# High and low weight parts in rows of eight instead of in turn, in an encoder block on one core

## The chip, the core and the metric

The kernel runs on one core of a Trainium2 chip. The metric is the device time of one execution in microseconds (us), as a median of several runs. The engines are named as the profile names them: PE is TensorE with its matmuls, PEld its weight loads, DVE is VectorE, ACT is ScalarE, POOL is GpSimd, SP is the queue that issues most transfers.

## The reference

One encoder layer on 256 tokens of width 2048, in f32, cut to the products that matter here:

```
h = rms_norm(x)
qa, ka, va, qb, kb, vb, ga, gb = split(h @ w_in)         # 2048 -> 10240 columns
ya = windowed attention(qa, ka, va)                       # 8 heads
yb = dilated attention(qb, kb, vb)                        # 12 heads, merged to 4
x  = x + (sigmoid(ga) * (ya @ w_branch_a) + sigmoid(gb) * (yb @ w_branch_b)) @ w_out
hf = rms_norm(x)
x  = x + (gelu(conv3(hf @ w_ffn_gate)) * (hf @ w_ffn_up)) @ w_ffn_down   # 2048 -> 5632 -> 2048
x  = x + sigmoid(rms_norm(x) @ w_ple_gate) * (p @ w_ple_proj)
out = rms_norm(x)
```

## The kernel before

**Two parts per number.** TensorE takes operands in a reduced f32 type here (`FR`), so each f32 operand is held as a high part and a low part, the low part being what the high part leaves over. A product of two such numbers is three matmuls: high by high, high by low, low by high.

**Two kinds of products.** In the first, weights are the moving operand (`wide_product`, L359 to L361, and `seven_product`, L410 to L412): 512 weight columns stream past a 128 by 128 block of activations. In the second kind, which the change concerns, a 128 by 128 weight block is the stationary operand and the activations move. For every block of weights `block` (L324 and L325) issues two matmuls into one PSUM accumulator `acc` of 128 by 512: the high part `whi` against 512 columns (256 tokens of the activations' high part, then 256 of their low part), and the low part `wlo` against the first 256 columns, added to the right half of `acc`. Later one ACT and one DVE operation (`gather`) add the halves. The left half is then high by high and the right half holds both mixed terms.

**Where that kind is used.** `product` does 16 blocks one after another for each head's query and key columns and for each 128 columns of the MLP's gate and up matrices. `products_by_halves` does the first three gate products together (`gg`): eight blocks of each of the three, then the other eight of each, so that half of the normalised input is enough to begin. Together these are 1840 blocks. Seven more products at the very start (tile `first`) call `block` themselves.

**How the weights come.** They lie in DRAM in the order of use. SP loads them in tiles of eight blocks (`raw`). `split_to` has ACT write `whi` (L261) and DVE write `wlo` (L262) for each tile of eight; there are four buffers of each. While the blocks of tile s are issued, `split_to(s + 3)` sees to it that tiles up to s + 2 are written in the program.

**What sets the order.** Each product has due times: `at((i, k), f)` puts a piece of other work (attention, norms, transposes) before block k of job i, and `run_due(i, k)` issues it there. So PE's order is that of the blocks with this other work between them; within ACT and DVE a scheduler that estimates durations orders what the program leaves free. The first product after the start is job `START` - 1, here called the first product; ahead of its block 6 stand the column sums for the first norm (L472), ahead of its block 12 the matmul that spreads the norm's factor over the partitions (L500, which needs POOL's power L486 and DVE's `rdg` L494). Transposes (`flip`, L878) turn the residual into the moving input `mov` (ACT L464, DVE L465); four of them lie in `gg` ahead of its blocks 8, 12, 16 and 20.

Of the kernel before, what the change touches and what calls it, by code (L numbers as in the profile page):

```python
# [17 lines left out]
T = 256  # L18
D = 2048
KC = D // P  # L20
# [17 lines left out]
SUB = 8  # L38
# [78 lines left out]
TOGETHER = 3  # L117
# [8 lines left out]
def _pairs(kind, c):  # L126

    if kind == "o":
        return ([2, 4, 5, 6, 7, 0, 1, 3] if c else [0, 1, 2, 4, 5, 6, 7, 3]), range(LATER, LATER + 4)
    if kind == "d1" and c == 1:  # L130
        return [5, 0, 1, 6, 2, 3, 7, 4, 8, 9, 10], range(5)
    return [8, 0, 1, 2, 3, 9, 4, 5, 6, 7, 10], range(SAVED)
# [34 lines left out]
def _whole(a):  # L167

    return _BLOCKS[a][0] == "w_out" or (_BLOCKS[a + SUB][1] % FHALF) // 2 in WHOLE
# [16 lines left out]
_SUB_OF = {a + o: (i, o) for i, (a, n, part) in enumerate(_SUBS) if not part for o in range(n)}  # L186
# [3 lines left out]
def _encoder(ctx: ExitStack, tc, xt, pt, cols, table, onehot, mask, ident_in, last_gain, wts, xrows, out):  # L190
    nc = tc.nc
# [34 lines left out]
    raws, subs = {}, {}  # L226
    pairs_of, kept = {}, {}
    state = {"raw": 0, "sub": 0, "at": 0, "back": 0}
# [12 lines left out]
    def load_all(i):  # L241
        while state["raw"] < min(i, 2 * _NPIECES):
            r, h = divmod(state["raw"], 2)
            seven = h and r * PIECE in _SEVEN
            load(r, h * SUB, h * SUB + (4 if seven else SUB))
            if seven and _whole(r * PIECE):
                nc.sync.dma_start(raws[2 * r + h][:, 4:, :], kept[_SEVEN.index(r * PIECE)][1])

    def split_to(i):
        while state["sub"] < min(i, len(_SUBS)):  # L250
            s = state["sub"]
            a, n, part = _SUBS[s]
            h, o = divmod(a, SUB)
            load_all(h + 6 + (part == 3))
            if part is None:
                src = raws[h][:, o:min(o + n, SUB), :]
            else:
                src = (raws[h + 1][:, :4, :], pairs_of.get(a), raws[h], raws[h + 1])[part]
            hi = wpool.tile(list(src.shape), FR, name="whi", bufs=4)
            lo = wpool.tile(list(src.shape), FR, name="wlo", bufs=4)  # L260
            nc.scalar.activation(hi, src, AF.Copy)  # L261
            ins = nc.vector.tensor_tensor(lo, src, hi.bitcast(F32), op=ALU.subtract)  # L262
            if _BLOCKS[a][0] in ("w_out", "w_ffn_down"):
                keep(ins)
            subs[s] = (hi, lo)
            state["sub"] = s + 1
            if part is not None:
                t2, t4 = raws[h + 1][:, 4:, :], raws[h + 1][:, :4, :]
            if part == 0 and not _whole(a):
                keep(nc.vector.tensor_tensor(t2, raws[h][:, :4, :], pairs_of[a][:, :4, :], op=ALU.subtract))  # L270
            if part == 1:
                keep(nc.vector.tensor_tensor(t4, raws[h][:, 4:, :], t2, op=ALU.subtract))
                j = _SEVEN.index(a)
                if all(not j <= e < j + 3 for e in _LAST):
                    back()
# [35 lines left out]
    def back():  # L311

        j = state["back"]
        t = pairs_of[_SEVEN[j]] = two_sums()
        nc.sync.dma_start(t, kept[j][0])
        state["back"] = j + 1

    def block(acc, m, first, last, ahead=3):

        b = state["at"]  # L320
        s, o = _SUB_OF[b]
        split_to(s + ahead)
        hi, lo = subs[s]
        nc.tensor.matmul(acc, hi[:, o, :], m, start=first, stop=False, skip_group_check=True)  # L324
        nc.tensor.matmul(acc[:, T:], lo[:, o, :], m[:, :T], start=False, stop=last, skip_group_check=True)  # L325
        state["at"] = b + 1
        if o == _SUBS[s][1] - 1:
            del subs[s]

    def product(i, moving, n):  # L330
        acc = ps.tile([P, 2 * T], F32, name="acc", bufs=3)
        for k in range(n):
            run_due(i, k)
            block(acc, moving(k), k == 0, k == n - 1)
        return acc

    def products_by_halves(i, moving):

        accs = []
        for b in range(TOGETHER * KC):  # L340
            (h, e), k = divmod(b // SUB, TOGETHER), b % SUB
            run_due(i, b)
            if h + k == 0:
                tag = "sp" if e < 2 else "acc"
                accs.append(ps.tile([P, 2 * T], F32, name="acc", tag=tag, bufs=2 if e < 2 else 3))
            block(accs[e], moving(SUB * h + k), h + k == 0, h == 1 and k == SUB - 1)
        return accs

    def wide_product(i, still, n, w, tag, places=HALVES, late=0):

        accs = [ps.tile([P, W4], F32, name="acc", tag=tag, bufs=3 if tag == "acc" else 2) for _ in places]

        def step(k, t, hi, lo):
            xh, xl = (still(k)[:, c:c + T][:, places[t]] for c in (0, T))
            acc = accs[t][:, :w * P]
            nc.tensor.matmul(acc, xh, hi, start=(k == 0), stop=False)  # L359
            nc.tensor.matmul(acc, xh, lo, start=False, stop=False)  # L360
            nc.tensor.matmul(acc, xl, hi, start=False, stop=(k == n - 1 - t * late))  # L361

        later = []
        for k in range(n):
            run_due(i, k)
            b = state["at"]
            s, o = _SUB_OF[b]
            split_to(s + 3)
            hi, lo = (m[:, o:o + w, :] for m in subs[s])
            step(k, 0, hi, lo)  # L370
            if k < n - late:
                step(k, 1, hi, lo)
            else:
                later.append((k, 1, hi, lo))
            state["at"] = b + w
            if o == _SUBS[s][1] - w:
                del subs[s]
        def rest(side=None):
            acc, c = (accs[1][:, :T], 0) if side is None else (side, T // P)
            for e, (k, t, hi, lo) in enumerate(later):  # L380
                xh, xl = (still(k)[:, c:c + T][:, places[t]] for c in (0, T))
                for i, (xs, ws) in enumerate(((xh, hi), (xh, lo), (xl, hi))):
                    nc.tensor.matmul(acc, xs, ws[:, c:c + T // P, :], start=(side is not None and e + i == 0),
                                     stop=(e + i == len(later) + 1), skip_group_check=True)
        return accs, rest
# [137 lines left out]
    def run_due(*i):  # L523
        for f, a in due.pop(i, []):
            f(*a)
# [48 lines left out]
    for step in order:  # L574
# [6 lines left out]
        while state["at"] < min(FIRST * ready, _SUBS[state["sub"]][0]):  # L581
            k, e = divmod(state["at"], FIRST)
# [15 lines left out]
    b = ps.tile([NH, 2 * T], F32, name="misc")  # L598
# [240 lines left out]
    def spread_sums(n, bank, end):  # L839

        u = row()
        nc.scalar.activation(u, bank["p1"], AF.Copy)  # L842
        to_residual(n, 0, 0, u)
        last = u
        for name in ("p6", "p7"):
            v = row()
            nc.vector.tensor_tensor(v, bank[name], last, op=ALU.add)
            last, u = v, last
        u, v = u, last
        to_residual(n, 1, 0, v)  # L850
        w = row()
        nc.vector.tensor_tensor(u, bank["p5"], u, op=ALU.add)
        nc.vector.tensor_tensor(w, bank["p5"], v, op=ALU.add)
        for t, a in enumerate((u, w)):
            if end:
                q = quarter(n, t, 1)
                nc.vector.tensor_tensor(q, q, a, op=ALU.add)
            else:
                to_residual(n, t, 1, a)
# [143 lines left out]
    for i, job in enumerate(_JOBS):  # L1003
        kind, n, _, _, _, blocks = job
# [79 lines left out]
        last = i == len(_JOBS) - 1  # L1084
        rest = None
        if kind == "v":
            far = n[0] >= KVH + HG
            acc, _ = wide_product(i, stills["v"], blocks, len(n), "acc", TWINS if far else HALVES)
        elif kind in ("o", "d0", "d1"):
# [5 lines left out]
            acc = seven_product(i, *_pairs(kind, n), still, lambda m, e: [a[:, e, :] for a in sums_at(m)], tags,  # L1095
                                lambda bank: spread_sums(n, bank, end))
        elif kind in stills:
            tag = {"pg": ("pt", "acc"), "pp": ("sp", "acc"), "gb": ("sp", "sp"), "ga": ("acc", "acc"), "ba": ("acc", "acc"),
                   "bb": ("sp", "sp" if n == 1 else "acc")}[kind][n % 2]
            acc, rest = wide_product(i, stills[kind], blocks, 4, tag, late=8 if last else 0)  # L1100
        elif kind == "gg":
            acc = products_by_halves(i, movers["g"])
        else:
            acc = product(i, movers[kind], blocks)
# [91 lines left out]
```

## Time and profile before

| what | value |
|---|---|
| median of 3 runs | 1469.22 us (1468.95 to 1469.9) |
| profiled execution, its own time | 1465.36 us |
| its span in the profile | 1463.6 us |
| granted TensorE clock, mean | 0.998 |
| PE busy | 1450.6 us, 99% of the span |
| weight loads busy | 1238.4 us, 85% |
| DVE busy | 1112.7 us, 76% |
| ACT busy | 816.2 us, 56% |
| traffic of the core's DMA engines | 362.17 MB, mean 247 GB/s |

A matmul's listed duration runs from its start to its modelled end, and matmuls overlap. What one costs the stream is therefore the step from its start to the start of the next one, not its listed duration. Such steps are read in the list of instructions in order of time, or from how many starts fall into a stretch in which PE does nothing else. The profiled execution is 3.86 us below the median of the timed runs.

### The profile page before, as it was taken

The numbers are of one execution on the slowest core, as the hardware profiler recorded it, in microseconds if no ns is written. First come the engines' busy times: TensorE is split into PE (matmuls) and PEld (weight loads), VectorE is DVE, ScalarE is ACT, GpSimd is POOL, SyncE is SP. The second block draws the span as 40 slices with busy tenths as digits, with TensorE's granted clock in tenths as the row PEclk, the third lists the DMA queues.
The fourth block names the chain that finished last, engine by engine and source line by source line (L and its number), as shares of the span: only waits on it lengthen the run. The fifth ranks groups of instructions, "written<-read, shape, count | busy, mean of one in ns | idle before, by whom it ended". The sixth has DMA issues, their size and how long they took to land.

```text
span 1463.6 us, 20762 instructions
## 1 busy us (share of the span) xinstructions
PE 1450.6 (99%) x7531; PEld 1238.4 (85%) x7531; DVE 1112.7 (76%) x1575; ACT 816.2 (56%) x1155; POOL 107.0 (7%) x178
## 2 busy tenths in 40 slices
PE   9999999999999999999999999999999999999997
PEld 8988888888888888788888887888888888788886
DVE  7686665665665668879888878897888876988665
ACT  7465444444444456666555555675555555666653
POOL 0000000001111100201011100102110100010000
PEclk9999999999999999999999999999999999999999
DMA  9654445557888977977788886989888874797652
GB/s 326 235 180 160 168 169 171 190 180 258 294 305 295 353 234 254 291 244 272 263 281 276 292 283 201 290 289 309 278 278 279 292 241 162 257 306 243 218 192 88
DMA packets 111730, 362.17 MB, mean 247 GB/s; under 512 B 12804, under 2 KB 17924, under 8 KB 111500
## 3 DMA queue, kind: packets, MB, share of 16 engines
q1 hardware_dynamic: 88908, 292.80, 58.2%
q0 software_dynamic: 20560, 63.71, 14.3%
q10 hardware_dynamic: 2160, 4.33, 0.9%
q8 instruction: 59, 0.97, 0.3%
q14 instruction: 43, 0.35, 0.1%
HBM read 324.06 MB, written 27.30 MB: 240 GB/s over the span
## 4 chain that ended last, share of the span: by engine, by line
PE 93%; DVE 1%; ACT 0%; issue 0%; POOLq 0%; POOL 0%; DVEq 0%
PE acc L324 28%; PE acc L325 14%; PE acc L360 9%; PE acc L359 9%; PE acc L361 9%; PE acc L411 7%; PE acc L410 7%; PE acc L412 7%; PE pt L685 1%; PE pt L878 0%; DVE wlo L262 0%; PE misc L700 0%; PE sp L644 0%; PE pt L900 0%; PE misc L631 0%
## 5 line engine op out<-in xcount | busy, mean ns | idle before, releaser
L262 DVE TENSOR_TENSOR wlo<-raw,whi 128x1024 fp32r<-128x1024 f32 (+2 forms) x556 | 650.9, 1182 | 289.2 <-ACT whi L261 284.2
L261 ACT ACTIVATE whi<-raw 128x1024 fp32r<-128x1024 f32 (+2 forms) x556 | 564.3, 1025 | 530.9 <-PE acc L324 191.0
L324 PE MATMUL acc<-mov,whi 128*128 128x512 f32 x1840 | 642.5, 394 | 0.0
L325 PE MATMUL acc<-mov,wlo 128*128 128x256 f32 x1840 | 514.2, 279 | 0.0
L324 PEld LDWEIGHTS acc<-mov,whi 128*128 128x128 f32 x1840 | 345.3, 188 | 76.9
L325 PEld LDWEIGHTS acc<-mov,wlo 128*128 128x128 f32 x1840 | 347.1, 189 | 0.3
L359 PE MATMUL acc<-whi,mov 128*128 128x512 f32 (+1 forms) x504 | 193.6, 384 | 0.0
L361 PE MATMUL acc<-whi,mov 128*128 128x512 f32 (+1 forms) x504 | 193.4, 384 | 0.0
L360 PE MATMUL acc<-wlo,mov 128*128 128x512 f32 (+1 forms) x504 | 193.3, 384 | 0.0
L359 PEld LDWEIGHTS acc<-whi,mov 128*128 128x128 f32 x504 | 95.2, 189 | 18.6 <-DVE first L452 0.5
L361 PEld LDWEIGHTS acc<-whi,mov 128*128 128x128 f32 x504 | 95.2, 189 | 18.5
L360 PEld LDWEIGHTS acc<-wlo,mov 128*128 128x128 f32 x504 | 95.2, 189 | 17.9
L410 PE MATMUL acc<-whi,act 128*128 128x512 f32 x207 | 80.9, 393 | 0.2 <-ACT whi L261 0.2
L411 PE MATMUL acc<-wlo,act 128*128 128x512 f32 x207 | 81.1, 392 | 0.0
L412 PE MATMUL acc<-whi,act 128*128 128x512 f32 x207 | 80.7, 390 | 0.0
L837 POOL DMA_DIRECT2D x<-row x36 | 31.0, 878 | 375.9 <-ACT row L842 255.3
L262 DVE TENSOR_TENSOR wlo<-sums,whi 128x1024 fp32r<-128x1024 f32 x37 | 45.2, 1220 | 8.5 <-ACT whi L261 8.4
L452 DVE TENSOR_TENSOR u<-acc,t 128x256 f32<-128x256 f32 x100 | 41.8, 418 | 8.4 <-ACT t L448 8.4
L410 PEld LDWEIGHTS acc<-whi,act 128*128 128x128 f32 x207 | 38.8, 188 | 9.4 <-ACT whi L261 1.5
L411 PEld LDWEIGHTS acc<-wlo,act 128*128 128x128 f32 x207 | 38.9, 188 | 9.2 <-DVE wlo L262 1.3
L411 PE MATMUL acc<-wlo,shl 128*128 128x512 f32 x116 | 45.7, 394 | 0.0
L412 PEld LDWEIGHTS acc<-whi,act 128*128 128x128 f32 x207 | 38.9, 188 | 7.9
(218 smaller groups left out, 1642.1 us busy)
## 6 DMA issues: line engine op xcount, KB each, us to landing
raw<-in_wts SPq DMA_DIRECT2D x477, 512.0 KB, 5.1
sums<-kept SPq DMA_DIRECT2D x37, 512.0 KB, 5.4
sums<-in_wts POOLq DMA_DIRECT2D x23, 512.0 KB, 7.9
kept<-sums POOLq DMA_DIRECT2D x23, 512.0 KB, 5.7
raw<-in_wts SPq DMA_DIRECT2D x39, 256.0 KB, 5.1
row<-in_wts POOLq DMA_DIRECT2D x37, 256.0 KB, 8.3
x<-row POOLq DMA_DIRECT2D x36, 256.0 KB, 7.6
two<-in_wts POOLq DMA_DIRECT2D x14, 512.0 KB, 8.2
```

The source lines that it names most:

```text
L261: nc.scalar.activation(hi, src, AF.Copy)
L262: ins = nc.vector.tensor_tensor(lo, src, hi.bitcast(F32), op=ALU.subtract)
L324: nc.tensor.matmul(acc, hi[:, o, :], m, start=first, stop=False, skip_group_check=True)
L325: nc.tensor.matmul(acc[:, T:], lo[:, o, :], m[:, :T], start=False, stop=last, skip_group_check=True)
L359: nc.tensor.matmul(acc, xh, hi, start=(k == 0), stop=False)
L360: nc.tensor.matmul(acc, xh, lo, start=False, stop=False)
L361: nc.tensor.matmul(acc, xl, hi, start=False, stop=(k == n - 1 - t * late))
L410: nc.tensor.matmul(acc, xh, hi, start=(e == 1), stop=False)
L411: nc.tensor.matmul(acc, xh, lo, start=False, stop=False)
L412: nc.tensor.matmul(acc, xl, hi, start=False, stop=(e == uses[name]))
L452: nc.vector.tensor_tensor(u, acc[:, :T], t, op=ALU.add)
L837: keep(nc.gpsimd.dma_start(quarter(n, t, c), a, accum_op=ALU.add))
```

## The change

`product` and `products_by_halves` no longer call `block` for each weight block. They call a new function `eight` for each tile of eight blocks. It issues the eight high matmuls and the eight low matmuls as two rows: for the first tile of a product high ones first, for a later tile low ones first. With 16 blocks to a product this gives 8 high, 16 low, 8 high, and since the next product begins with high again, rows of 16 of each in the middle of a stage. `eight` keeps due work at the same number of matmuls: it is called ahead of every second matmul, so what stood before block k of a tile now stands before the tile's matmul 2k. The products at the very start and both kinds with moving weights are as they were.

```diff
     def product(i, moving, n):
         acc = ps.tile([P, 2 * T], F32, name="acc", bufs=3)
-        for k in range(n):
-            run_due(i, k)
-            block(acc, moving(k), k == 0, k == n - 1)
+        for g in range(n // SUB):
+            eight(acc, lambda k: run_due(i, SUB * g + k), lambda k: moving(SUB * g + k), g == 0, g == n // SUB - 1)
         return acc

+    def eight(acc, due_at, moving, first, last):
+
+        s, _ = _SUB_OF[state["at"]]
+        for p in range(2 * SUB):
+            if p % 2 == 0:
+                due_at(p // 2)
+                split_to(s + 3)
+            hi, lo = subs[s]
+            k = p % SUB
+            m = moving(k)
+            if (p < SUB) == first:
+                nc.tensor.matmul(acc, hi[:, k, :], m, start=(first and k == 0), stop=(last and k == SUB - 1),
+                                 skip_group_check=True)
+            else:
+                nc.tensor.matmul(acc[:, T:], lo[:, k, :], m[:, :T], start=False, stop=False, skip_group_check=True)
+        state["at"] += SUB
+        del subs[s]
+
     def products_by_halves(i, moving):

         accs = []
-        for b in range(TOGETHER * KC):
-            (h, e), k = divmod(b // SUB, TOGETHER), b % SUB
-            run_due(i, b)
-            if h + k == 0:
+        for g in range(2 * TOGETHER):
+            h, e = divmod(g, TOGETHER)
+            if h == 0:
                 tag = "sp" if e < 2 else "acc"
                 accs.append(ps.tile([P, 2 * T], F32, name="acc", tag=tag, bufs=2 if e < 2 else 3))
-            block(accs[e], moving(SUB * h + k), h + k == 0, h == 1 and k == SUB - 1)
+            eight(accs[e], lambda k: run_due(i, SUB * g + k), lambda k: moving(SUB * h + k), h == 0, h == 1)
         return accs
```

The new lines move what follows down by 16: L472 becomes L488, L500 becomes L516, L465 becomes L481, and the two matmuls of `block` are L347 (high) and L350 (low) in these products.

In the first product PE's order before, around the column sums (`tot` holds the summed squares), is this:

```order
L324 MATMUL acc<-mov,whi 128x512
L325 MATMUL acc<-mov,wlo 128x256
L472 MATMUL misc<-ones,tot 128x1 x4
L324 MATMUL acc<-mov,whi 128x512
L325 MATMUL acc<-mov,wlo 128x256
```

In the changed kernel the same product, from its first matmul to the first rows of the next, stands so:

```order
L347 MATMUL acc<-mov,whi 128x512 x8
L350 MATMUL acc<-mov,wlo 128x256 x4
L488 MATMUL misc<-ones,tot 128x1 x4
L350 MATMUL acc<-mov,wlo 128x256 x12
L516 MATMUL misc<-rdg,ones 128x256
L347 MATMUL acc<-mov,whi 128x512 x16
```

The sums stand behind 8 high and 4 low matmuls instead of 6 and 6, and the spreading matmul behind 8 high and 16 low instead of 12 and 12.

In `gg`, PE's order in the changed kernel, with the four transposes (L894, L878 before) between the rows:

```order
L347 MATMUL acc<-mov,whi 128x512 x8
L350 MATMUL acc<-mov,wlo 128x256 x8
L894 MATMUL pt<-ident,x 128x128 x4
L347 MATMUL acc<-mov,whi 128x512 x8
L894 MATMUL pt<-ident,x 128x128 x4
L350 MATMUL acc<-mov,wlo 128x256 x8
L347 MATMUL acc<-mov,whi 128x512 x3
L894 MATMUL pt<-ident,x 128x128 x4
L347 MATMUL acc<-mov,whi 128x512 x5
L350 MATMUL acc<-mov,wlo 128x256 x4
L894 MATMUL pt<-ident,x 128x128 x4
L350 MATMUL acc<-mov,wlo 128x256 x18
```

The last transposes stand behind 24 high and 20 low matmuls, where before 20 high and 20 low ones stood ahead of them in this product; the row of 18 behind them takes 4 of its low matmuls from the third tile, 8 from the fourth and 6 from the fifth.

DVE's order around the same transposes, before (`mov` is the moving input, `rdg` the diagonal of the norm's factors):

```order
L262 TENSOR_TENSOR wlo<-raw,whi 128x1024 x2
L465 SCALAR_TENSOR_TENSOR mov<-pt,cl,mov 128x256 x4
L262 TENSOR_TENSOR wlo<-raw,whi 128x1024
L465 SCALAR_TENSOR_TENSOR mov<-pt,cl,mov 128x256 x4
L262 TENSOR_TENSOR wlo<-raw,whi 128x1024
L478 TENSOR_REDUCE sum<-marks 128x2
```

And in the changed kernel:

```order
L262 TENSOR_TENSOR wlo<-raw,whi 128x1024 x2
L481 SCALAR_TENSOR_TENSOR mov<-pt,cl,mov 128x256 x3
L262 TENSOR_TENSOR wlo<-raw,whi 128x1024
L481 SCALAR_TENSOR_TENSOR mov<-pt,cl,mov 128x256 x4
L262 TENSOR_TENSOR wlo<-raw,whi 128x1024
L481 SCALAR_TENSOR_TENSOR mov<-pt,cl,mov 128x256
```

The eighth piece of `mov` moved behind one more `wlo`. Elsewhere ACT and DVE keep the same instructions with some neighbours exchanged; POOL's order is the same, and SP's differs by the place of a few loads.

## The prediction

> **What bounds the kernel now.** I read the page's totals first, then the waits of PE, then PE's list in order of time, since the question is what one matmul costs the stream.
>
> ```profile
> span 1463.6 us, 20762 instructions
> PE 1450.6 (99%) x7531; PEld 1238.4 (85%) x7531; DVE 1112.7 (76%) x1575; ACT 816.2 (56%) x1155; POOL 107.0 (7%) x178
> PEclk9999999999999999999999999999999999999999
> L324 PE MATMUL acc<-mov,whi 128*128 128x512 f32 x1840 | 642.5, 394 | 0.0
> L325 PE MATMUL acc<-mov,wlo 128*128 128x256 f32 x1840 | 514.2, 279 | 0.0
> ```
>
> PE is busy from end to end at full clock, and the two matmuls of the change show no idle time ahead of them. So the kernel is as long as PE's stream of starts, and the change, which only reorders 3680 of PE's 7531 matmuls, must act through the steps between starts, or through new waits. The mean durations, 394 and 279 ns, are no steps: their ends are modelled and they overlap.
>
> ```profile
> 799.88 0.39 PE L324 MATMUL acc<-mov,whi 128*128 128x512 f32 x1
> 799.88 0.19 PEld L325 LDWEIGHTS acc<-mov,wlo 128*128 128x128 f32 x1
> 800.11 0.27 PE L325 MATMUL acc<-mov,wlo 128*128 128x256 f32 x1
> 800.11 0.19 PEld L324 LDWEIGHTS acc<-mov,whi 128*128 128x128 f32 x1
> 800.22 0.40 PE L324 MATMUL acc<-mov,whi 128*128 128x512 f32 x1
> ```
>
> In turn, high to low is 0.23 us and low to high 0.11 us, some 0.345 a pair. Each weight load starts together with the matmul before the one that uses it: the load for a high matmul lies beneath the short low one. For a mean over many pairs I count starts of L324 in stretches; the columns are the stretch, its length, PE's busy time with the count of starts, and the loads.
>
> ```profile
> core 0: us, PE busy (x) PEld busy (x), PEclk, DMA share, GB/s
> 186.00:210.00 24.00, 24.00 (x69) 12.80 (x68) 1.00 0.56 190
> 162.00:228.00 66.00, 50.16 (x142) 26.71 (x142) 1.00 0.50 168
> 246.00:284.00 38.00, 29.89 (x84) 15.82 (x84) 1.00 0.54 181
> 636.00:660.00 24.00, 19.81 (x55) 10.36 (x55) 1.00 0.57 201
> 1040.00:1200.00 160.00, 160.00 (x463) 86.50 (x462) 1.00 0.82 276
> ```
>
> In the MLP (last row) 160 us hold 463 starts, the one at the edge counted in, or 160 / 461.5 = 346.7 ns a pair. In a part of the head projections (first row) it is 24 / 68 = 353 ns, at the same clock and with less traffic: a slower rhythm of the same alternation, without any wait on another engine.
>
> **What the rows will cost.** The kernel already has both kinds of rows, each matmul with its own weight load: the last gate product runs 512 columns after 512, the first value product and the last gate's remainder 256 after 256. The first two lines are 36 steps apart, the next two 95, the next two 46, and the last two 95.
>
> ```profile
> 1439.99 0.39 PE L361 MATMUL acc<-whi,mov 128*128 128x512 f32 x1
> 1448.15 0.39 PE L361 MATMUL acc<-whi,mov 128*128 128x512 f32 x1
> ...
> 47.61 0.28 PE L360 MATMUL acc<-wlo,mov 128*128 128x256 f32 x1
> 59.00 0.40 PE L324 MATMUL acc<-mov,whi 128*128 128x512 f32 x1
> ...
> 1448.49 0.28 PE L383 MATMUL acc<-wlo,mov 128*128 128x256 f32 x1
> 1454.01 0.28 PE L383 MATMUL acc<-whi,mov 128*128 128x256 f32 x1
> ...
> 228.88 0.40 PE L359 MATMUL acc<-whi,mov 128*128 128x512 f32 x1
> 251.04 0.40 PE L361 MATMUL acc<-whi,mov 128*128 128x512 f32 x1
> ```
>
> A 512-column step is 8.16 / 36 = 226.7 ns. A 256-column step is 11.39 / 95 = 119.9 ns and 5.52 / 46 = 120.0 ns. Their sum is 346.7 ns, which is the alternating pair of the MLP to a tenth of a nanosecond. So a step's price goes by the matmul's own columns and not by its neighbour: 256 columns more cost 106.7 ns, and each matmul pays about 13.3 ns besides, in a row as in alternation. This is the core of the forecast: **rows cost what the turns cost**. (The last two lines, 22.16 / 95 = 233.3 ns, are a value product whose stationary operand takes every second column; they come back below.)
>
> One thing goes: if the rows run at 346.7 a pair everywhere, the slow rhythm ends. The three stretches that contain it hold 142, 84 and 55 high matmuls, at most 281 x (353 - 346.7) = 1.8 us; not all of them beat slowly, and I take **-1.6 us**. The bounds for the rhythm are -1.8 us and, were all 1840 high matmuls to step at 233.3, 1840 x 6.6 = +12.1 us. I take the near end, since of the 512-column rows the contiguous one, as the weight blocks here are, steps at 226.7.
>
> A rule of the Trainium skill (TensorE: Matmul & The Clock Gate, LDWEIGHTS) speaks against rows of low parts: a load takes as long as its columns last at 1.2 GHz, by an estimate from it 128 / 1.2 = 107 ns, all but the whole streaming time of 256 columns, and such a row has no long matmul to make up for it. By that figure the sum stays as it is, as 107 is below the 120 measured here with a load for every matmul; the trace agrees.
>
> **What the moved work costs.** Due work stands behind the same number of matmuls, not the same time, and shifts by up to 0.45 us (four high ones for low ones: 4 x 106.7 ns). Where PE meets this work with little to spare, it now waits. I looked at three places. The first is the first product, 59.00 us on:
>
> ```profile
> 61.13 0.97 PE L472 MATMUL misc<-ones,tot 128*128 128x1 f32 x8
> 61.96 0.48 PE L324 MATMUL acc<-mov,whi 128*128 128x512 f32 x1
> 62.13 0.16 DVE L484 TENSOR_SCALAR rv<-misc 128x4 f32<-128x4 f32 x1 [0.61 <-PE misc L472]
> 62.38 1.02 POOL L486 TENSOR_TENSOR rr<-rv,mhalf 128x4 f32<-128x4 f32 x1 [61.93 <-DVE rv L484]
> 63.43 0.48 DVE L494 TENSOR_SCALAR rdg<-ident,rr 128x128 f32<-128x128 f32 x2 [1.13 <-POOL rr L486]
> 64.16 0.60 PE L500 MATMUL misc<-rdg,ones 128*128 128x256 f32 x2
> ```
>
> The sums come after 8 x 0.2267 + 4 x 0.12 = 2.29 us instead of 61.13 - 59.00 = 2.13: 0.16 later, and the chain to `rdg` with them, ready at 63.91 + 0.16 = 64.07. PE reaches the spreading matmul after the sums (61.29 + 0.83), the restart behind them (the high matmul at 61.96 lists 0.48 us for some 0.39: 0.09) and twelve low matmuls (1.44): 63.65. It waits some 0.4 us, where before it came 0.25 after `rdg`; with the signal's way I take **+0.5** (0 to 0.8). Second, the first head's softmax (L673) and its transposes (L685):
>
> ```profile
> 76.61 0.61 DVE L673 TENSOR_SCALAR s<-s,rd 128x256 f32<-128x256 f32 x2
> 76.65 0.28 PE L325 MATMUL acc<-mov,wlo 128*128 128x256 f32 x1
> 77.01 0.33 PE L685 MATMUL pt<-ident,s 128*128 128x128 f32 x1
> ```
>
> PE already stood here for 0.36 - 0.12 = 0.24 us, with DVE working without a break. These transposes are due ahead of block 11: 3 pairs into the second tile, now 6 low matmuls, so 8 pairs plus 0.72 = 3.49 instead of 11 x 0.3467 = 3.81 us. PE comes 0.32 earlier, DVE a little later by the first place, whose own wait gives part of it back: **+0.4** (0 to 0.8). Third, `gg`:
>
> ```profile
> 646.96 0.60 PE L878 MATMUL pt<-ident,x 128*128 128x128 f32 x4
> 647.55 2.06 DVE L465 SCALAR_TENSOR_TENSOR mov<-pt,cl,mov 128x256 fp32r<-128x256 f32 x4
> 647.60 1.50 ACT L464 ACTIVATE mov<-pt,cl 128x256 fp32r<-128x256 f32 x3 [0.79 <-PE pt L878]
> 648.81 0.40 PE L324 MATMUL acc<-mov,whi 128*128 128x512 f32 x1
> ```
>
> The fourth tile starts at 648.81 and used its last input 7 pairs later, at 651.2, with ACT done at 649.10 and DVE at 649.61. Now the last transposes come 4 high matmuls later (0.91), ACT is done near 650.0, and the tile's low row, which reads ACT's half alone, wants its last input 0.84 us after its start, at about 649.6: **+0.4** (0 to 1.0). DVE's half is wanted by the high row behind the eight low ones and six more, about 652, when even a DVE that does one `wlo` more ahead of it is done.
>
> Elsewhere the weights are no new limit. A pair of `whi` and `wlo` is asked for three tiles ahead:
>
> ```profile
> ACT whi L261 <- PE acc L324: 194.2, 159, 3.4
> 799.26 1.06 ACT L261 ACTIVATE whi<-raw 128x1024 fp32r<-128x1024 f32 x1 [1.44 <-PE acc L324]
> 800.36 1.23 DVE L262 TENSOR_TENSOR wlo<-raw,whi 128x1024 fp32r<-128x1024 f32 x1 [0.25 <-ACT whi L261]
> ```
>
> ACT waited 194.2 us for PE to free buffers, not PE for ACT; a tile begun at 799.26 is whole at 801.59, 2.3 us later, against three tiles of 2.77 us.
>
> **The sum:** -1.6 + 0.5 + 0.4 + 0.4 = -0.3 us, a span of 1463.3 us. The profiled execution is 1465.36 us, or 1.8 above its span, and the median 3.9 above that; I add the difference to the median: **1468.9 us**.
>
> **The rivals.**
>
> Slower, the rhythm: the rows of high matmuls fall into the slow step. The point is 2.9 us / 6.6 ns = 440 of the 1840; with all, 1469.2 + 12.1 = 1481 us. For it: the alternation does it in three stretches, and one 512 row of the kernel steps at 233.3. Against it: that row has a strided stationary operand, and the contiguous row shows nothing of it.
>
> Slower, the low part first: from a product's second tile on, `wlo` is wanted before anything else, 0.23 us earlier than in turn. Were DVE late with it, each of some 100 rows of 16 low matmuls would stall by that, 23 us, 1492 us; it decides from 13 rows on. Against it stand the three tiles of lead.
>
> Faster: steps in a row come out shorter than the kernel's present rows, by the 1.6 ns a pair (2.9 us / 1840) that would show, or the restarts vanish as well; near 1465 us. For it, the alternation's slow rhythm proves that order can matter to a step; against it, two 256 rows at 120 and the MLP at 346.7. Were 13.3 ns beside the columns to fall to a fourth in rows, it would be 1840 x 2 x 10 = 37 us, 1432 us. The Trainium skill (TensorE: Matmul & The Clock Gate, Back-to-back issue gap) has just such a price, N / 2.4 + 2.5 ns, by an estimate 325 ns for a pair and some 40 us less; the trace disagrees, with its own rows at 346.7.
>
> That the change doesn't do what it says is out: the changed order has rows of 16 nearly everywhere.
>
> **How the numbers follow.** A measurement of this kernel tells about 0.2%, 2.9 us, from no change. The forecast, no change that can be told, has 0.70. The slow rhythm has 0.08, the late low part with other new waits together 0.07: slower 0.15. Shorter steps have 0.15, of which 0.02 for the far case. Range: below, -1.6 without any of the waits is 1467.6, and the near faster case 1465; above, the three waits at their upper ends, 2.6 - 1.6 = +1.0, and part of the slow rhythm up to 5 us: **1464.5 to 1474 us**.
>
> **What would show it.** In the profile after: starts of the high matmul 227 ns apart within a row and of the low one 120; 160 us of the MLP still worth 461 blocks; the head projections at 346.7 a block, without 353; PE waiting for `rdg` at the spreading matmul, longer at the first transposes, and for ACT's `mov` in `gg`, each under 1 us. High rows at 233, low rows under 115 or over 125, or stalls at the turn to a low row through the MLP would make it wrong.

## The result, and the profile after

Thirteen executions of each kernel, taken together, give 1468.14 us before (1462.89 to 1469.9) and 1464.0 us with the change (1461.91 to 1465.75). The ratio is **0.9977, 95% interval 0.9966 to 0.9987**: a gain of 0.23%, at the edge of what can be told. The two profiled executions hardly differ: 1465.36 us before, 1464.53 us after, spans of 1463.6 and 1462.7 us. So most of the gain is not in the pair of profiles the forecast was made from, and that is where the experiments begin: single executions of the kernel before fall into two groups, near 1464 and near 1468 us, and those of the changed kernel into one.

The page of the changed kernel, lines that answer to those shown of before:

```profile
span 1462.7 us, 20616 instructions
PE 1449.0 (99%) x7531; PEld 1242.1 (85%) x7531; DVE 1110.8 (76%) x1575; ACT 818.1 (56%) x1155; POOL 107.1 (7%) x178
L347 PE MATMUL acc<-mov,whi 128*128 128x512 f32 x1840 | 441.6, 391 | 0.0
L350 PEld LDWEIGHTS acc<-mov,wlo 128*128 128x128 f32 x1840 | 237.3, 191 | 9.1 <-ACT mov L480 0.2
L350 PE MATMUL acc<-mov,wlo 128*128 128x256 f32 x1840 | 242.8, 283 | 0.0
```

The busy sums of the two matmuls are now 441.6 and 242.8 us where they were 642.5 and 514.2. That is no gain: a modelled end no longer reaches into a neighbour of the other line. The steps say what it costs. PE's list in the MLP of the changed kernel:

```profile
1054.22 3.82 PE L347 MATMUL acc<-mov,whi 128*128 128x512 f32 x16
1057.87 2.08 PE L350 MATMUL acc<-mov,wlo 128*128 128x256 f32 x16
1059.78 1.55 PE L347 MATMUL acc<-mov,whi 128*128 128x512 f32 x6
```

Sixteen high and sixteen low take 1059.78 - 1054.22 = 5.56 us here. By the unrounded starts in the trace, the 81 such double rows of the two halves take 5566.7 ns on average, 347.9 ns a pair against 346.7 in turn. The 1.2 ns more lie where a high row begins. The steps from one start to the next, as means over the rows of the first half (680 to 860 us):

```
high row   233.3 235.9 228.3 232.5 230.8, then eleven of 226.7
low row    113.3 119.2, then fourteen of 120.0
```

The first five high steps are 27 ns dearer together and the first two low ones 7.5 ns cheaper, so a high row and a low row cost 0.02 us more than the same matmuls in turn.

By windows, all engines, the columns being stretch, length, and for each engine in the page's order its busy time with the count of starts:

```profile
680.00:860.00 180.00, 180.00 (x1036) 159.06 (x1035) 154.01 (x257) 101.35 (x155) 20.53 (x38) 1.00 0.84 281
1040.00:1200.00 160.00, 160.00 (x923) 141.48 (x923) 137.29 (x228) 90.50 (x136) 15.67 (x29) 1.00 0.82 274
```

Both halves of the MLP step alike in the changed kernel. With rows, a count of starts depends also on where the window cuts a row: the further profile of the changed kernel below (run a1) has the same steps and counts 1040 in the first window.

```profile
680.00:860.00 180.00, 180.00 (x1040) 159.25 (x1039) 154.05 (x256) 101.00 (x153) 20.04 (x37) 1.00 0.83 282
```

So rows are compared here by their steps, and only turns by counts. That the two halves do not always step alike before is the next section's matter.

### The profile page after: what moved, and what is told of

Read it like the earlier page. It is cut to its first block, busy times and chain, and to the rows that moved or that the text cites. A ratio compares the mean times of both kernels' runs of the same rounds, so it can differ in the third digit from the quotient of the medians.

```text
span 1462.7 us, 20616 instructions
## 1 busy us (share of the span) xinstructions
PE 1449.0 (99%) x7531; PEld 1242.1 (85%) x7531; DVE 1110.8 (76%) x1575; ACT 818.1 (56%) x1155; POOL 107.1 (7%) x178
## 4 chain that ended last, share of the span: by engine, by line
PE 95%; issue 2%; DMA 1%; DVE 1%; ACT 0%; SPq 0%; POOLq 0%; POOL 0%; DVEq 0%; ACTq 0%
PE acc L347 29%; PE acc L350 15%; PE acc L375 9%; PE acc L377 9%; PE acc L376 9%; PE acc L427 6%; PE acc L428 6%; PE acc L426 6%; PE first L324 2%; PE first L325 1%; DMA x<-row 1%; PE pt L894 1%; PE pt L701 0%; DMA raw<-in_wts 0%; PE sp L660 0%
## 5 line engine op out<-in xcount | busy, mean ns | idle before, releaser
L347 PE MATMUL acc<-mov,whi 128*128 128x512 f32 x1840 | 441.6, 391 | 0.0
L347 PEld LDWEIGHTS acc<-mov,whi 128*128 128x128 f32 x1840 | 337.8, 188 | 65.5
L350 PEld LDWEIGHTS acc<-mov,wlo 128*128 128x128 f32 x1840 | 237.3, 191 | 9.1 <-ACT mov L480 0.2
L350 PE MATMUL acc<-mov,wlo 128*128 128x256 f32 x1840 | 242.8, 283 | 0.0
L464 ACT ACTIVATE t<-acc 128x256 f32<-128x256 f32 x115 | 43.9, 382 | 132.6 <-PE acc L347 132.6
L805 ACT ACTIVATE c<-c 128x256 f32<-128x256 f32 x44 | 18.3, 417 | 57.3 <-DVE c L804 57.3
L426 PEld LDWEIGHTS acc<-whi,act 128*128 128x128 f32 x207 | 38.8, 188 | 8.8 <-ACT whi L261 0.9
```

Source lines behind the costliest of these rows:

```text
L347: nc.tensor.matmul(acc, hi[:, k, :], m, start=(first and k == 0), stop=(last and k == SUB - 1), skip_group_check=True)
L350: nc.tensor.matmul(acc[:, T:], lo[:, k, :], m[:, :T], start=False, stop=False, skip_group_check=True)
L426: nc.tensor.matmul(acc, xh, hi, start=(e == 1), stop=False)
L464: keep(nc.scalar.activation(t, acc[:, T:], AF.Copy, scale=scale))
```

## The experiments

### The kernels themselves, profiled again

The first four runs change nothing. They ask where the executions of one kernel differ.

> The kernel before, unchanged, profiled once more, to see why its executions spread over 7 us (1462.89 to 1469.9) and those of the change over 4 us. Theory A (rhythm): in turn, the pairs of high and low sit in one of two rhythms, 346.7 or 353 ns a pair, and which one is an accident of each execution; an execution near 1468 has some 400 to 700 pairs more in the slow rhythm than the profiled 1465.36 us one, so stretches of the MLP (680 to 860 us, 1040 to 1200 us) show 353 ns in a part of them. Theory B (waits): the pairs are at 346.7 ns in the MLP in every execution, and the difference lies in waits of PE for whi and wlo at the starts of the down projection (near 893 and 1248 us, 1.9 us in the first profile) and other places, which vary. Theory C: it lies at the start, before 60 us, in the time to the first weights.

> As the run before it: a third execution of the kernel before. By theory A its span less that of the first profile (1463.6 us) is the number of pairs more in the slow rhythm times 6.6 ns, to within 0.5 us; by theory B it is the difference of PE's waits with all pairs at 346.7 ns; by theory C it is the time of the first matmul with stationary weights of the first product (59.0 us in the first profile).

> As the two before it: a fourth execution of the kernel before, same expectations by theories A, B and C.

> The changed kernel, unchanged, profiled once more. Theory A: rows at 226.7 and 120 ns again in the MLP, 160 us worth the same number of starts as in its first profile, the span within 2 us of 1462.7. Theory B: the same rows, and the waits at the starts of the down projection again under 0.3 us, where the first profile of the kernel before had 1.9 us. Theory C: the difference to 1462.7 us stands before 60 us.

The three further executions of the kernel before took 1469.77, 1467.59 and 1468.1 us, the changed kernel's 1462.73. Starts of the high matmul in the first half of the MLP (680 to 860 us), in the profile that the forecast used:

```profile
680.00:860.00 180.00, 180.00 (x520) 97.50 (x520) 1.00 0.82 280
```

with 463 in the second half, as shown there, and in the first of the further ones (L324 alone: starts, then loads):

```profile
680.00:860.00 180.00, 180.00 (x511) 95.75 (x510) 1.00 0.81 272
1040.00:1200.00 160.00, 160.00 (x463) 86.37 (x462) 1.00 0.83 278
```

511 instead of 520 starts in 180 us: 353 ns a pair instead of 346.7, at clock 1.00, and the trace lists no wait of PE or of its loads in this stretch. All three have 510 or 511, and 462 or 463 in the second half. Over the whole trace the excess of the pairs over 346.7 ns (pairs with an interruption left out) is 1.62 us in the forecast's profile and 6.06, 6.06 and 6.09 us in the three. That is theory A: the slow rhythm is an accident of the execution, and the forecast's profile was one of the luckier ones. The spans are 4.4, 2.2 and 2.7 us above that profile's, where the rhythm alone makes 4.4 to 4.5, so the agreement to 0.5 us that was expected holds in the first of the three only. Theory C has a part here, under 1.5 us: the first matmul behind the start stage comes at 45.9 to 47.4 us in the six profiles of both kernels, latest in the forecast's; in the three further ones it comes 0.7, 1.5 and 1.1 us earlier than there. With both counted, some 0.7 us stay unexplained in each of the three, up in the first and down in the others.

Theory B is true as well, but of the change and not of the scatter. PE's loads at the start of the first down projection waited, in the forecast's profile of the kernel before,

```profile
PEld acc L411 <- DVE wlo L262: 1.4, 4, 0.4
PEld acc L410 <- ACT whi L261: 0.3, 1, 0.3
```

1.7 us in 5 waits, in the further profiles of it 1.9 to 2.0 us in 6, but in the two of the changed kernel 0.7 us in 4 short ones and 0.2 us in one:

```profile
PEld acc L427 <- DVE wlo L262: 0.7, 4, 0.2
```

### One instruction moved by one pair

The first half's products run undisturbed from the spreading matmul L500 (656 us) to the down projection, so whatever rhythm follows L500 lasts 220 us. The steps ahead of L500, from the unrounded starts in the trace (ns; h is high to low, l is low to the next high, the last l is the step into L500):

```
forecast's profile  h235 l114 h232 l118 h241 l120  L500   then 346.7 a pair
b1                  h241 l120 h235 l114 h232 l119  L500   then 353
b2                  h240 l120 h236 l114 h232 l118  L500   then 353
b3                  h241 l120 h235 l114 h232 l119  L500   then 353
```

The slow rhythm is a beat of three (241, 235, 232). Where L500 falls behind the 232, the slow rhythm goes on after it. The test moves that one matmul (two instructions in the trace), in the kernel before:

```diff
-            rms([(i, 36), (i + 1, 2), (_HALF + 1, 9)], lambda: rowsums(held["ss1"]), 1, 2)
+            rms([(i, 36), (i + 1, 3), (_HALF + 1, 9)], lambda: rowsums(held["ss1"]), 1, 2)
```

> The kernel before, with one PE instruction moved: the matmul that spreads the second norm's factor (L500, near 656 us) stands one pair of high and low matmuls later, ahead of block 3 instead of block 2. Rhythm theory: alternation keeps the rhythm it has until something interrupts it, and which one it has afterwards depends on the beat of the three-beat rhythm (steps of 241, 235 and 232 ns from high to low) on which the interruption falls. In the three further profiles L500 fell behind the 232 beat and 353 ns followed for 220 us; behind the 241 beat, one pair later, 346.7 ns should follow: 519 or 520 starts of L324 from 680 to 860 us instead of 510 or 511, and 4.4 us less, about 1463.5 us, ratio 0.997, with no row of high or low anywhere. Rival (rows): the gain of the change comes from rows themselves or from the order on ACT and DVE; then one moved instruction does nothing, 510 starts, ratio 1.000.

**Measured: 1463.75 us** (ten executions, 1463.26 to 1464.8, all in the lower group), ratio 0.9973, interval 0.9959 to 0.9987, with ACT's, DVE's, POOL's and SP's orders untouched. All engines in the first half (PE's starts of both kinds first):

```profile
680.00:860.00 180.00, 180.00 (x1040) 157.38 (x1039) 154.40 (x257) 100.74 (x153) 19.98 (x38) 1.00 0.83 282
```

That is 520 pairs.
One moved matmul gives what the whole change gives, without a single row. The rival that rows as such are the gain falls here. In the same group of runs, 19 of the 31 executions of the kernel before took 1467.6 us or more, and the other 12 at most 1466.2.

### Rows of two

```diff
-            k = p % SUB
+            k = 2 * (p // 4) + p % 2
...
-            if (p < SUB) == first:
+            if (p % 4 < 2) == first:
```

> The changed kernel with rows of two instead of eight: high, high, low, low, and so on, with the two orders in turn from tile to tile as in the change. Rhythm theory, if it is strict turns that lock into 353 ns: no lock, 519 or 520 pairs in 180 us of the MLP, about 1464 us, ratio 0.997 to 0.998. Rival (switches cost): the step after a switch from low to high is dearer, as 0.02 us a product in the change suggests; with four times the switches 0.08 us more a product, 7 to 9 us over 115 products, and a ratio of 1.002 to 1.004. Rival (short rows lock too): 510 pairs, ratio 1.000.

**Measured: 1466.1 us**, ratio 0.9986, interval 0.9972 to 1.0. The counts of all engines in the same windows:

```profile
680.00:860.00 180.00, 180.00 (x1033) 157.45 (x1032) 155.29 (x256) 102.81 (x153) 20.50 (x38) 1.00 0.83 280
1040.00:1200.00 160.00, 160.00 (x918) 139.94 (x917) 137.77 (x229) 91.71 (x137) 15.67 (x29) 1.00 0.81 274
```

The steps of these 180 us exceed 226.7 ns for each high and 120.0 for each low matmul by 1.3 us, and in the second half by 1.1 us in 160, the same rate. With rows of eight it is 0.6 to 0.7 us in each half, with turns in the 346.7 ns rhythm nothing, and with turns at 353 ns 3.4 us in the first half. So short rows show no lock either, and a switch between the rows costs something, but less than feared: 0.04 us a product, against 0.02 with rows of eight.

### Rows in the first half alone, and everywhere else

The edit, in both: a job goes to `eight` if a condition holds, and to the old loop over `block` if not. Shown is the condition of the first kernel; the complement has `not (...)` around it.

```diff
+    def rows_at(i):
+        kind, n = _JOBS[i][0], _JOBS[i][1]
+        return kind in ("g", "u") and n < FHALF
```

> Rows of eight in the gate and up products of the MLP's first half alone (650 to 880 us), turns everywhere else, the three first gate products included. Rhythm theory: 4.4 us less than before from the first half, less 0.02 us for each of some 41 products, 0.8: ratio 0.9975. The head projections keep their 353 ns stretches. The waits of PE for whi and wlo at the start of the first down projection (1.4 us before, 0.2 in the change) go if they hang on the rows just ahead of it, those at the second down projection (0.7 us) stay. Rival (order): the gain comes from the head projections and the starts; ratio 0.9995 or above.

> The complement: rows of eight everywhere but in the gate and up products of the MLP's first half, which stay in turn. Rhythm theory: the first half locks into one of the two rhythms by accident of the beat: at 353 ns the ratio is 0.999 to 1.000 (some 1.5 us less for the other stretches, 0.6 less for the second down projection's waits, 1 us more for switches and the two waits of the changed order), at 346.7 ns it is near 0.996. The start counts from 680 to 860 us tell which, 510 or 520. Rival (order): 0.998, with the gain outside the first half and 510 starts in it.

Rows in the first half alone: **1464.2 us**, ratio 0.9977 (0.9964 to 0.9991), the whole of the change's gain. Rows everywhere else: **1468.18 us**, ratio 1.0 (0.9987 to 1.0014), none of it, with every one of its ten executions at 1467.47 or above. The first kernel's windows, then the complement's:

```profile
680.00:860.00 180.00, 180.00 (x1041) 159.35 (x1040) 154.06 (x257) 101.34 (x153) 19.98 (x38) 1.00 0.83 281
1040.00:1200.00 160.00, 160.00 (x925) 141.18 (x924) 136.17 (x228) 89.60 (x137) 15.07 (x28) 1.00 0.82 275
```

```profile
680.00:860.00 180.00, 180.00 (x1021) 156.24 (x1020) 152.87 (x252) 98.07 (x150) 20.52 (x38) 1.00 0.82 273
1040.00:1200.00 160.00, 160.00 (x918) 141.33 (x918) 137.17 (x230) 89.89 (x137) 15.65 (x29) 1.00 0.81 276
```

The complement's first half, in turn, sits at 353 ns (1021 starts of both kinds, some 510 pairs). Its second half, in rows, counts 918 where turns have 925, but by the steps it is 0.6 us in 160 that the rows cost, as in the changed kernel. Its ten executions are all slow: L500 stands two pairs behind a row there, and in the profile it falls behind a high step of 232 ns. The waits at the two down projections follow the rows just ahead of them. At the first one, rows in the first half leave one wait:

```profile
PEld acc L441 <- DVE wlo L262: 0.2, 1, 0.2
```

and the same kernel keeps 1.4 us in 5 waits at the second, where its products are in turn; the complement has 1.2 us in 4 waits at the first and 0.3 us in 2 at the second.

### The beat once more: two and three pairs later

> The kernel before with the spreading matmul L500 moved by two pairs, ahead of block 4. Rhythm theory in its sharp form (353 ns follows only where L500 falls behind the 232 beat of the three): of 31 executions of the kernel before, 19 were slow (1467.6 to 1471.2) and 12 fast (up to 1466.2), so block 2 lies behind the 232 beat in some 6 of 10 executions and, by the first profile, behind the 241 beat in the others. Block 3 then lies behind 241 or 235, never slow, as the run with one pair showed (10 of 10 below 1465). Block 4 lies behind 235 or, in some 4 of 10, behind 232: so again two groups, 4.5 us apart, but with the fast one the larger: some 3 to 5 of 10 executions at 1468 to 1470, the others at 1463 to 1465, median near 1464.5. Rival (the later place simply suits the norm's chain): all executions fast as with one pair, 1463.8. Rival (no memory of the beat): the same split as the kernel before, 6 of 10 slow.

```diff
+            rms([(i, 36), (i + 1, 4), (_HALF + 1, 9)], lambda: rowsums(held["ss1"]), 1, 2)
```

**Measured: 1464.23 us**, ten executions from 1463.29 to 1465.83, ratio 0.9986 (0.9972 to 0.9999). None near 1469, where some four were expected: the theory in that form missed. The last two runs ask what was open, whether the beat decides at all.

```diff
+            rms([(i, 36), (i + 1, 5), (_HALF + 1, 9)], lambda: rowsums(held["ss1"]), 1, 2)
```

> The kernel before with the spreading matmul L500 three pairs later, ahead of block 5. The sharp form of the rhythm theory fell in one point: block 4 was never slow in 10 executions, where 4 were expected. What is left of it: the rhythm ahead of L500 repeats every three pairs, so block 5 meets the same beat as block 2, and the kernel should split as the kernel before does (33 of 52 slow in the two groups of runs), 5 to 8 of 10 executions at 1467.6 to 1471 and the others at 1463 to 1466. Rival (distance: the earlier L500 comes, the likelier the slow rhythm, whatever the beat): none of 10 slow, as at blocks 3 and 4.

> The kernel before, profiled a fifth time. If it is a slow execution (above 1467.5 us), L500 stands behind the 232 beat of the three and 353 ns follow until 880 us. If it is a fast one (below 1466.5), L500 stands behind another beat, as in the first profile (241), or meets the 346.7 ns rhythm, in which there are no three beats; the second would explain why no execution with L500 at block 4 was slow.

Three pairs later, **six of ten executions are back at 1467.57 to 1468.93 us**, the other four at 1462.95 to 1465.06; median 1467.74, ratio 0.999 (0.9978 to 1.0002). Two pairs later none, one pair later none, three pairs later as in the kernel before: the period is three, and the rival that a later place is simply better falls. (Two pairs later leaves the orders of ACT and DVE as they were; three pairs later exchanges a few neighbours there.) Starts of the high matmul in the first half, two and three pairs later:

```profile
680.00:860.00 180.00, 180.00 (x521) 97.13 (x520) 1.00 0.83 281
680.00:860.00 180.00, 180.00 (x511) 95.88 (x510) 1.00 0.81 274
```

The fifth profile of the kernel before happened to be one of the lower group (1462.73 us) and shows what the miss was about. Steps ahead of L500 as above:

```
one pair later      h236 l112 h234 l116 h242 l120  L500   then 346.7
two pairs later     h232 l118 h240 l120 h236 l115  L500   then 346.7
three pairs later   h240 l121 h236 l113 h233 l118  L500   then 353
b4                  h230 l116 h229 l118 h230 l116  L500   then 346.7
```

In b4 the 346.7 ns rhythm was there already ahead of L500; its steps there differ by 1 to 2 ns only, so L500 would find no beat of 241 or 232 ns to fall behind, wherever it stands. If the lower group of the kernel before is mostly of that kind, two pairs later is never slow, as measured. The forecast's own profile (L500 behind the 241) is of another kind, by which two pairs later should meet the 232 now and then; ten executions had none. How often each kind comes, and what sets the rhythm ahead of L500, stays open.

### A version that beats both

Only where a profile showed a gain does it use rows; L500 stands one pair later.

```diff
...
+        if kind in ("k", "q"):
+            return n >= (QH if kind == "q" else KVH)
+        return kind == "u" and n % FHALF == FHALF - 1
...
-            rms([(i, 36), (i + 1, 2), (_HALF + 1, 9)], lambda: rowsums(held["ss1"]), 1, 2)
+            rms([(i, 36), (i + 1, 3), (_HALF + 1, 9)], lambda: rowsums(held["ss1"]), 1, 2)
```

> A version meant to beat both: the kernel before with L500 one pair later, which keeps the MLP's turns at 346.7 ns, and rows of eight only where a profile showed a gain of theirs: in the query and key products of the dilated heads (0.9 us less in their 353 ns stretches) and in the last up product of each half of the MLP (PE's waits for whi and wlo at the two down projections, 1.1 and 0.5 us less, if the rows just ahead of them do it). Rhythm theory: no switches through the MLP, so 2.0 to 2.5 us below the run with L500 one pair later: a span near 1459.3 us and a median near 1461.5, ratio 0.9955. If the waits at the down projections need more than the last product in rows, 1462.9. Rival (rows themselves are the gain): 1467 to 1468, since most of the MLP is in turn again.

**Measured: 1461.5 us** (eleven executions, 1460.48 to 1462.21), ratio 0.9962, interval 0.9948 to 0.9976; the changed kernel's median, from another group of runs, is 2.5 us above. Its page and the two down projections' waits, the first and the second:

```profile
span 1460.0 us, 20754 instructions
...
L324 PE MATMUL acc<-mov,whi 128*128 128x512 f32 x1424 | 495.6, 393 | 0.0
```

```profile
PEld acc L443 <- DVE wlo L262: 0.2, 1, 0.2
...
PEld acc L443 <- DVE wlo L262: 0.5, 3, 0.2
```

1424 of the 1840 blocks are in turn again, and 416 in rows; one product in rows ahead of each down projection is enough to bring its waits to 0.2 and 0.5 us. The gain over the kernel with L500 alone moved (1463.75 us) was taken between two groups of runs, and which of the rows gives how much of it was not tested singly.

## Why the prediction was right or wrong

The forecast was no change that can be told, 1468.9 us, with 1464.5 to 1474; measured were a ratio of 0.9977, which makes 1465.8 us of the 1469.22 shown then, and a median of 1464.0 us, half a microsecond below the range. The direction was missed by a little: the gain is 0.23% where 0.2% was the line.

**Rows cost what turns cost: right, to 0.4%.** 226.7 and 120 ns were read from other rows; the changed kernel's MLP steps 347.9 ns a pair. That a switch between the rows costs something (0.02 us for a high and a low row, by the first steps of each shown above) was not seen; over the span, at 0.02 us for each of 115 products, it takes back some 2.3 us, an estimate.

**The slow rhythm, -1.6 us: the term that failed.** The mechanism was right, that rows end the 353 ns rhythm, but it was sized from one profile, with 1.62 us of it. In three of the four further profiles it is 6.1 us. The forecast had the warning in hand: the profiled execution lay 3.9 us below the median, and "I add the difference to the median" carried that over as if it were a constant. Nothing asked what the median execution did that the profiled one did not; the 4.4 us of slow rhythm in the first half of the MLP, in three of the four further profiles, are of that size. The bound of -1.8 us was wrong for the same reason: it counted the stretches of one execution.

**The spreading matmul of the first norm, +0.5 us: right.** In the changed kernel:

```profile
61.62 1.68 PE L350 MATMUL acc<-mov,wlo 128*128 128x256 f32 x12
63.72 0.67 PE L516 MATMUL misc<-rdg,ones 128*128 128x256 f32 x2 [0.42 <-DVE rdg L510]
```

PE waits 0.42 us for `rdg`, just as the sum of twelve low steps said, and its stream loses 0.58.

**The first head's transposes, +0.4 us: wrong in sign.** They start without a wait at 76.54 us:

```profile
76.54 0.62 PE L701 MATMUL pt<-ident,s 128*128 128x128 f32 x4
```

The wait at the spreading matmul held PE back by 0.58 us, while the transposes came 0.32 earlier in its order; the 0.24 us of standing before are gone as well. From 74 to 79 us the steps are 0.4 us shorter than before, not longer. I had named that one wait gives the other back, and then added both.

**`gg`, +0.4 us: right in size.** Above their own price (26.7 ns for each 64 columns and 13.3 ns besides), PE's steps between 640 and 680 us take 1.7 us in the change's first profile and 1.1 in the forecast's, 0.6 more; part of it is the low row that waits for ACT's `mov` (the 0.2 us in the page's row above).

**Not in the sum: the down projections.** The loads' waits at the second one, in the forecast's profile and then in the change's:

```profile
PEld acc L411 <- DVE wlo L262: 1.2, 4, 0.3
PEld acc L410 <- ACT whi L261: 0.3, 1, 0.3
...
PEld acc L427 <- DVE wlo L262: 0.3, 2, 0.2
```

Loads wait 1.0 us less at the first (shown above) and 1.2 less at the second in the two profiles, which is 1.05 and 0.8 us of PE's steps above their own price. The rows just ahead cause it, by the two complementary kernels; why the weights are ready earlier there was not settled.

Against its own profile the change gained 0.9 us, and -0.3 was the sum. With the sizes measured it is -1.6 + 0.6 - 0.4 + 0.6 from the forecast's terms, +2.3 for the switches and -1.9 for the down projections, -0.4 us in all; the start came 0.5 us earlier besides. That the sum came near is luck in part: two terms that were not in it nearly cancel. Against the executions the change gained 4.1 us by the medians. Of the rivals, the slow rhythm in rows, at 233 ns, shows in the first five steps of each high row and not beyond, and the late low part did not show; the faster one, "near 1465 us", came true, but by the rhythm and not by shorter steps.

## What to carry to other kernels

A profile is one execution. When its time lies off the median of the runs by more than the effect one forecasts, the profile's own deviation has to be explained first, by further profiles of the same kernel. And count starts per stretch, stage by stage: this stream ran 2% slow for 220 us at full clock, with no wait in any view. Where matmuls of different length stand in rows, compare the time of whole rows instead, since a window that cuts a row changes the count by itself (1036 and 1040 for the same steps here).

## What the runs showed of the hardware that was not expected

Alternating matmuls of 512 and 256 columns, each with its own weight load, have two steady rhythms, 346.7 ns a pair and a three-pair beat of 353 ns on average (steps from high to low of 241, 235 and 232 ns). The stream stays in the one it has until other PE work interrupts it, here for 220 us at a time, and the interruption's place within the beat decides which follows: behind the 232 ns step in all five profiles that went on at 353 (three of the kernel before, three pairs later, rows everywhere else), behind another beat or from the even rhythm in all five that went on at 346.7 (two of the kernel before, one and two pairs later, the last version). Why the beat decides is not shown. Rows of two or of eight show no such lock.

The gap that the Trainium skill gives for an isolated matmul (TensorE: Matmul & The Clock Gate, Back-to-back issue gap: N / 2.4 + 2.5 ns, 216 ns for 512 columns) was reached in no row here, each with a weight load per matmul: 226.7 and 120.0 ns differ by 106.7 ns for 256 columns, as N / 2.4 in the Trainium skill has it, and leave 13.3 ns besides in both.
